# A cumulative sum behind a matrix product: the first 4 MB brought by hardware queues as float32

## The chip, the cores and the metric

The kernel runs on one core of a Trainium2 chip. The metric is device time in microseconds (us) of the whole launch, lower is better. Matrix work runs on TensorE (PE in the profile, its weight loads PEld), vector work on VectorE (DVE), ScalarE (ACT) and GpSimd (POOL). Transfers are issued by SyncE (SP) and ScalarE on hardware queues, and by GpSimd on a software queue that can also cast float32 to bf16 on the way.

## What is computed

```python
B, S, D = 16, 2048, 1024          # x: B x S x D, w: D x D, decay: D, all float32
xw = x @ w
out[:, 0, :] = xw[:, 0, :]
for t in range(1, S):
    out[:, t, :] = decay[None, :] * out[:, t - 1, :] + xw[:, t, :]
```

## The kernel before

x is cut along time into 64 chunks of TL = 512 steps. A chunk arrives as bf16 in `xb` (four transfers by GpSimd, one for each 32 partitions), is turned in 32x32 blocks on VectorE into `xw` (`turn`) and copied into `xt` (`part`), which is the moving operand of the matmuls. w lies in `wsb` as bf16, 8 blocks k of the contraction times 8 blocks n of output columns. Chunks are taken in pairs. A step of the main loop is one n for one pair: 8 k's, 128 x 512 matmuls into PSUM, then the scan over time on VectorE (half of the tiles with help of ScalarE and GpSimd), a turn back and a store by SyncE. What each engine does in which order is written out by hand in `agenda`, a string of letters for each step. A letter calls the function that `deeds` gives it, and `pin` holds each instruction behind the one before it in program order on its own engine.

The change lies in the opening, the entry -99 of `agenda` and the lines ahead of it. There w's two column halves (h) and x's first two chunks come in. In w, rows with an even k belong to e = 0 and with an odd k to e = 1, so (h, e) names a quarter of w, 1 MB in float32. The staging room is the memory of two output tiles, `room[0]` and `room[1]` (so the profile calls these tiles `ot`).

- Lines 339 to 341: SyncE and ScalarE each bring 128 full rows of x (float32, 512 KB): the first half of chunk 0, in `whole`.
- `U0` to `U3` (`load_part`, `load_w`, line 323): GpSimd brings a quarter of w, cast to bf16, in four transfers. `M1` to `M3` (`load_half`, `load`, line 105): GpSimd brings half a chunk of x in four transfers; M1 is the second half of chunk 0, M2 and M3 are chunk 1. GpSimd's order is U0, I1, M1, U1, M2, M3, U2, U3 (I1 makes the unit matrix `eye`), then the loads `L` of later chunks.
- `H` and `J` (`gather`, line 376): VectorE and ScalarE cast the float32 rows to bf16 and reorder them into `upright`. `t0` to `t3` (`erect`, line 386): TensorE transposes them, 4 x 128x128 each, into a PSUM bank (`bed`). `o` and `O` (`lay`, line 393): VectorE and ScalarE copy them to `xt`.
- Line 354: TensorE runs 12 matmuls on zeros (`spin`) at the start. `K0` to `K3` (`spin_on`, line 404): when a piece of w's first quarter is in, ScalarE copies one column into a gate tile, and TensorE runs two or three more spins that need it.
- `W` and `w` (`settle_one`, line 330), `q` and `Q` (line 419): VectorE and ScalarE copy staged w into `wsb`.
- `n0` and `n1` (`begin`): 16 matmuls of 256 columns each, even k's, on the first and on the second half of chunk 0. The second half was turned on VectorE (`E4` to `E7`).
- Step 0 of the loop then runs the odd k's of chunk 0 (16 matmuls of 512 columns), then all k's of chunk 1.
- `D` makes the decay columns from `rows` (line 356, four small transfers by SyncE).

Of the kernel before, what the change touches and what calls it, by code (L numbers as in the profile page):

```python
# [9 lines left out]
FP32 = mybir.dt.float32  # L10
BF16 = mybir.dt.bfloat16
# [3 lines left out]
def _ap(ap_obj: bass.AP, new_ap, extra_offset=0):  # L15
    return dataclasses.replace(
        ap_obj,
        ap=[list(p) for p in new_ap],
        offset=ap_obj.offset + extra_offset,
    )  # L20
# [5 lines left out]
def kernel(  # L26
# [26 lines left out]
    nc = tc.nc  # L53
    pin = tc.keep_in_program_order
    B, S, D = x.shape
    assert w.shape == (D, D)

    NQ = 4
    P = 32
    CQ = D // NQ  # L60
    K = CQ // P
    M = K // 2
    TL = 512
    NJ = TL // P
    NC = S // TL
    R = K // 2
    CH = D // 2
    CR = CH // NQ

    const = ctx.enter_context(tc.tile_pool(name="const", bufs=1))  # L70
    sb = ctx.enter_context(tc.tile_pool(name="sb", bufs=1))
# [4 lines left out]
    def ring(pool, name, count, shape, dtype=FP32):  # L76
        i = turns[name] = turns.get(name, -1) + 1
        return pool.tile(shape, dtype, name=f"{name}{i % count}")

    def quad(q):  # L80
        return slice(q * P, (q + 1) * P)
# [12 lines left out]
    def ot_tile(nj):  # L94
        return ring(sb, "ot", 4, [128, nj, CR])

    xb_of = {}
    xw_of = {}
    xt_of = {}
# [25 lines left out]
    def matmul(ps, n, k, xt, t0=0, t1=TL, start=0, pairs=None):  # L125
        if pairs is None:
            rhs = xt[:, k // 2, k % 2, t0:t1]
        else:
            rhs = pairs[:, k // 2, t0 // P:t1 // P, :, k % 2].rearrange("p j i -> p (j i)")
        lhs = wsb[:, k, n].rearrange("p q i -> p (q i)")  # L130
        pin(nc.tensor.matmul(  # L131
            out=ps[:, t0:t1] if ps.shape[1] >= t1 else ps,
            lhsT=lhs,
            rhs=rhs,
            start=(k == 0 and t0 == start),
            stop=(k == K - 1),
        ))
# [3 lines left out]
    class Tile:  # L141
# [39 lines left out]
        def copy(self):  # L181
            self.xs = sb.tile([128, 2 * TL], FP32, name=f"xs{self.lot % 3}")[:, 0:self.T]
            parts = self.ps if isinstance(self.ps, tuple) else (self.ps,)
            size = self.T // len(parts)
            for i, ps in enumerate(parts):
                pin(nc.scalar.copy(out=self.xs[:, i * size:(i + 1) * size], in_=ps))  # L186
# [103 lines left out]
    class Outlet:  # L290
# [8 lines left out]
        def store(self, b, t0, j0, j1):  # L299
# [4 lines left out]
            for j in range(j0, j1, nj):  # L304
# [8 lines left out]

    room = [ot_tile(2 * NJ).rearrange("p j c -> p (j c)") for _ in range(2)]
    size = M * CH
    stage = {(0, 0): room[0][:, 0:size // 2].bitcast(BF16),
             (0, 1): room[0][:, size:size * 3 // 2].bitcast(BF16),
             (1, 0): room[1][:, 0:size // 2].bitcast(BF16),
             (1, 1): room[1][:, size // 2:size].bitcast(BF16)}

    def load_w(queues, h, e):
        for i, q in enumerate((0, 2, 1, 3)):
            pin(queues[i % len(queues)].dma_start(  # L323
                out=stage[h, e][quad(q)].rearrange("p (m d) -> p m d", m=M),
                in_=_ap(w, [[2 * D, P], [2 * P * D, M], [1, CH]],
                        (q * CQ + e) * D + h * CH)))

    def settle(h, e, m, copy):
        src = stage[h, e][:, m * CH:(m + 1) * CH]
# [3 lines left out]
    idle = const.tile([128, TL], BF16, name="idle")  # L333
    spare = ring(psp, "spare", 1, [128, TL])
    rows = const.tile([128, 2, P], FP32, name="rows")
    touch = const.tile([128, 1], BF16, name="touch")
    H = NJ // 2
    halves = ((0, H), (H, NJ))
    whole = room[1][:, size:2 * size].rearrange("p (u c) -> p u c", u=2)
    for u, queue in enumerate((nc.sync, nc.scalar)):  # L340
        pin(queue.dma_start(out=whole[:, u], in_=_ap(x, [[D, 128], [1, D]], u * 128 * D)))
    pin(nc.vector.memset(idle, 0.0))  # L342
    pin(nc.vector.memset(rows, 0.0))
    pin(nc.scalar.copy(out=touch, in_=idle[:, 0:1]))

    gates = [const.tile([128, 128], BF16, name=f"gate{q}") for q in range(NQ)]
    for gate in gates:
        pin(nc.vector.memset(gate, 0.0))

    def spin(count, by):  # L350
        for _ in range(count):
            pin(nc.tensor.matmul(out=spare, lhsT=by, rhs=idle, start=True, stop=True))  # L352

    spin(12, idle[:, 0:128])
    for q in range(NQ):
        pin(nc.sync.dma_start(
            out=rows[q * P:q * P + R],
            in_=_ap(decay, [[P, R], [CH, 2], [1, P]], q * CR)))
    cols = const.tile([128, 2, P], FP32, name="cols")

    def load_half(i):
# [5 lines left out]
    firsts = [ps[:, 0:TL] for ps in heads] + [spares[0]]  # L367
    seconds = [ps[:, TL:2 * TL] for ps in heads] + [spares[1]]
    eye = const.tile([128, 128], BF16, name="eye")

    upright = room[0][:, size * 3 // 2:2 * size].bitcast(BF16).rearrange(
        "p (e u m c) -> p e u m c", e=2, u=2, m=M)

    def gather(i, copy):
        e, u = i // 2, i % 2
        pin(copy(out=upright[:, e, u].rearrange("p m (q i) -> p m q i", q=NQ),
                 in_=whole[:, u].rearrange(
                     "p (q m i e) -> p e m q i", q=NQ, m=M, e=2)[:, e]))

    def bed(e):  # L380
        return seconds[e].bitcast(BF16).rearrange("p (m t) -> p m t", m=M)

    def erect(i):
        e, u = i // 2, i % 2
        for m in range(M):
            pin(nc.tensor.transpose(
                out=bed(e)[:, m, u * 128:(u + 1) * 128], in_=upright[:, e, u, m], identity=eye))

    def lay(i, copy):
        e, m = i // 2, i % 2 * 2  # L390
        if 0 not in xt_of:
            xt_of[0] = ring(sb, "xt", 5, [128, M, 2, TL], BF16)
        pin(copy(out=xt_of[0][:, m:m + 2, e, 0:H * P], in_=bed(e)[:, m:m + 2]))

    def begin(i):
        for k in range(0, K, 2):
            for n in range(R):
                if i == 0:
                    matmul(firsts[n], n, k, xt_of[0], 0, H * P)
                else:  # L400
                    matmul(firsts[n], n, k, xt_of[0], H * P, TL, pairs=xw_of[0])

    def spin_on(q):
        pin(nc.scalar.copy(out=gates[q][quad(q), 0:1], in_=stage[0, 0][quad(q), 0:1]))
        spin(3 if q == 0 else 2, gates[q])

    def load_part(i):
        load_w((nc.gpsimd,), i // 2, i % 2)

    def part_one(i, copy):  # L410
        part(i // 8, copy, i % 4, i % 4 + 1, *halves[i // 4 % 2])
# [106 lines left out]
    def turn_and_load(c):  # L518
# [16 lines left out]
        "w": lambda i: settle_one(i, nc.scalar.copy),  # L535
        "M": load_half,
        "U": load_part,
        "E": lambda i: turn(i // 8, *halves[i // 4 % 2], i % 4, i % 4 + 1),
        "F": lambda i: part_one(i, nc.vector.tensor_copy),
        "G": lambda i: part_one(i, nc.scalar.copy),  # L540
        "K": spin_on,
        "t": erect,
        "H": lambda i: gather(i, nc.vector.tensor_copy),
        "J": lambda i: gather(i, nc.scalar.copy),
        "O": lambda i: lay(i, nc.scalar.copy),
        "o": lambda i: lay(i, nc.vector.tensor_copy),
        "n": begin,
        "q": lambda i: settle_slots(i, 0, 1),
        "Q": lambda i: settle_slots(i, 1, R),
# [19 lines left out]
        "L": lambda i: load(*loads.pop(0)) if loads else None,  # L569
    }  # L570
    agenda = {
        -99: "U0 I1 M1 U1 M2 M3 U2 U3 H0 J1 t0 t1 H2 J3 t2 t3 O1 o0 K0 O3 o2 K2 K1 K3 W0 W1 w2 W3 n0 E4 E5 G4 E6 G5 E7 F6 G7 n1 q4 w5 Q4 W6 W7 D E8 E9 G8 E10 G9 E11 F10 G11 E12 L E13 G12 L E14 G13 E15 L F14 G15",
        0: "p0 z0 W8 W9 W10 W11",
        1: "g0",
        2: "L S1 L",
# [88 lines left out]
    for step, (g, n) in enumerate(slots):  # L664
        T = TL * len(g)
        left = step - len(slots)
        if n % R == 0:
            ns, nj = range(n, n + R), T // P
            if left == -2 * R:
                outlets = [Outlet(ns, H, half) for half in range(2)]  # L670
            else:
# [4 lines left out]
        if step == 0:  # L676
# [3 lines left out]
            for k0 in range(0, K, 2):  # L680
                for i in range(R):
                    for k in (k0, k0 + 1):
                        matmul(seconds[i], i, k, xt_of[1], 0, H * P,
                               pairs=xw_of[1] if k0 < 4 else None)
            for i in range(R):
                for k in range(K):
                    matmul(seconds[i], i, k, xt_of[1], H * P, TL, H * P,
                           pairs=xw_of[1] if i < 2 else None)
        if step < R:
            ps = heads[n] if n < 3 else tuple(spares)  # L690
        else:
# [16 lines left out]
            elif step == K:  # L708
                todo = []
                nexts = (ring(psp, "spare", 1, [128, TL]), ring(psp, "ps", 3, [128, TL]))  # L710
                for l in range(len(g)):
                    for i, half in enumerate((ps[:, l * TL:(l + 1) * TL], nexts[l])):
                        for k in range(K):
                            matmul(half, n + i, k, xt_of.get(g[l]),
                                   pairs=xw_of[g[l]] if g[l] in (3,) else None)
# [51 lines left out]
```

## Time and profile before

| | |
|---|---|
| median of 3 runs | 904.07 us (903.53 to 904.18) |
| the profiled execution | 903.72 us |
| its span on the core | 901.9 us |
| PE busy | 891.2 us, 99% of the span |
| DVE, ACT, POOL busy | 823.5, 687.1, 657.2 us |
| first matmul of `begin` | 9.95 us |
| start of step 0's odd k's | 14.97 us |
| first out transfer of SyncE | about 38.4 us |

Times inside the kernel count from the start of the span. The span is what the instructions of the core cover; the rest of the profiled execution's time lies around it. In the timelines a row has the start, the time to the end of the last instruction merged into it, the engine, the line, what it writes and reads, how many, and in brackets how long the engine was idle before and what released it.

### The profile page before, as it was taken

Reading aid. Unit: us, or ns where it says so; the run is one execution under the profiler, and the core shown is the slowest. Engines: PE = TensorE matmul, PEld = TensorE weight load, DVE = VectorE, ACT = ScalarE, POOL = GpSimd, SP = SyncE. Lnnn points to the kernel's source line nnn. Section 1 sums busy time; section 2 is a strip of 40 time slices with the busy share of each in tenths; the row PEclk is TensorE's granted clock in tenths of the full one; section 3 lists DMA queues with packets and bytes.
Section 4 is the critical chain, followed back from the end, with each engine's and each line's share of the span. In section 5 each row is a group of like instructions: output and inputs, shape, how many; then the busy total and the mean of one; then the engine's idle time right before and its main releaser. Section 6 shows DMA issues by size and latency. Waiting matters only on the chain.

```text
span 901.9 us, 12229 instructions
## 1 busy us (share of the span) xinstructions
PE 891.2 (99%) x4131; PEld 411.9 (46%) x4213; DVE 823.5 (91%) x636; ACT 687.1 (76%) x962; POOL 657.2 (73%) x757
## 2 busy tenths in 40 slices
PE   8999999999999999999999999999999999999998
PEld 5544444444444444444444444444444444444444
DVE  4999998989999999999998999999999999999998
ACT  4889867778877877878778778777787787787743
POOL 8888678768767768677677687777777776876532
PEclk9999999999999999999999999999999999999999
DMA  9999999999999999999999999999999999999868
GB/s 193 195 215 218 229 212 207 216 233 247 247 248 255 248 255 252 246 254 250 222 235 228 218 236 227 233 226 227 232 230 227 227 236 222 226 228 221 177 153 231
DMA packets 402382, 204.77 MB, mean 227 GB/s; under 512 B 9360, under 2 KB 401552, under 8 KB 402320
## 3 DMA queue, kind: packets, MB, share of 16 engines
q1 hardware_dynamic: 265664, 134.77, 60.8%
q0 software_dynamic: 136512, 68.70, 56.8%
q8 instruction: 33, 0.54, 0.2%
q10 hardware_dynamic: 144, 0.52, 0.1%
q14 instruction: 29, 0.24, 0.1%
HBM read 138.42 MB, written 134.22 MB: 302 GB/s over the span
## 4 chain that ended last, share of the span: by engine, by line
PE 97%; DMA 1%; issue 1%; POOL 0%; DVE 0%; ACT 0%; DVEq 0%; POOLq 0%
PE ps L131 96%; PE spare L131 1%; DMA ot<-in_w_dram 1%; POOL ot L323 0%; DVE so L233 0%; PE ps L460 0%; PE spare L460 0%; ACT xb L467 0%; DVE wsb L419 0%; DVEq L419 0%; POOLq L751 0%
## 5 line engine op out<-in xcount | busy, mean ns | idle before, releaser
L131 PE MATMUL ps<-xt,wsb 128*128 128x512 bf16 (+1 forms) x3946 | 862.6, 378 | 4.7 <-DVE wsb L419 0.4
L131 PEld LDWEIGHTS <-wsb 128*128 128x128 bf16 x4160 | 406.5, 98 | 479.8 <-issue 0.9
L208 POOL TENSOR_TENSOR xs<-h,xs 128x512 f32<-128x512 f32 (+1 forms) x190 | 242.7, 1278 | 184.1 <-ACT h L169 83.1
L283 DVE STREAM_TRANSPOSE ot<-so 128x1024 f32<-128x1024 f32 (+2 forms) x265 | 300.2, 1171 | 6.5 <-DMA out_dram<-ot 4.4
L186 ACT COPY xs<-ps 128x1024 f32<-128x1024 f32 (+1 forms) x190 | 188.8, 994 | 149.3 <-PE ps L131 137.5
L266 POOL TENSOR_TENSOR so<-h,xs 128x512 f32<-128x512 f32 (+1 forms) x190 | 241.2, 1271 | 46.9 <-ACT h L169 27.2
L123 ACT COPY xt<-xw 128x2048 bf16<-128x2048 bf16 (+1 forms) x133 | 240.6, 1816 | 9.5 <-DVE xw L115 9.5
L105 POOL DMA_DIRECT2D xb<-in_x_dram x260 | 171.6, 661 | 2.9 <-DMA ot<-in_w_dram 0.9
L169 ACT ACTIVATE h<-so,dec 128x512 f32<-128x512 f32 (+1 forms) x190 | 145.3, 766 | 32.8 <-DVE so L213 29.9
L115 DVE STREAM_TRANSPOSE xw<-xb 128x2048 f32<-128x2048 f32 (+1 forms) x74 | 145.9, 1981 | 6.5 <-DMA xb<-in_x_dram 6.5
L213 DVE TENSOR_TENSOR_SCAN so<-spare,keep,xs 128x512 f32<-128x512 f32 (+1 forms) x97 | 119.8, 1237 | 25.9 <-POOL xs L208 25.6
L213 DVE TENSOR_TENSOR_SCAN so<-spare,xs 128x512 f32<-128x512 f32 x93 | 113.0, 1217 | 25.4 <-POOL xs L208 22.8
L169 ACT ACTIVATE h<-ps,dec 128x512 f32<-128x512 f32 (+1 forms) x189 | 129.3, 684 | 0.0
L233 DVE TENSOR_TENSOR_SCAN so<-dec,ps 128x1024 f32<-128x1024 f32 x34 | 76.9, 2260 | 0.8 <-ACT h L169 0.6
L233 DVE TENSOR_TENSOR_SCAN so<-dec,keep,ps 128x1024 f32<-128x1024 f32 (+2 forms) x35 | 74.7, 2138 | 0.0
L270 ACT COPY keep<-so 128x1 f32<-128x1 f32 x136 | 25.2, 188 | 9.1 <-DVE so L233 8.7
L204 ACT COPY so<-keep 128x1 f32<-128x1 f32 x97 | 18.4, 191 | 2.6 <-DVE ot L283 2.4
L131 PE MATMUL spare<-xt,wsb 128*128 128x512 bf16 (+1 forms) x68 | 14.0, 329 | 0.0
L323 POOL DMA_DIRECT2D ot<-in_w_dram x16 | 9.0, 561 | 2.9 <-POOLq L751 0.9
L202 POOL MEMSET so<- 128x1 f32 x93 | 10.7, 116 | 0.6 <-DVE ot L283 0.6
L131 PE MATMUL ps<-xw,wsb 128*128 128x256 bf16 (+1 forms) x56 | 9.3, 307 | 0.8 <-DVE xw L115 0.8
L352 PE MATMUL spare<-idle 128*128 128x512 bf16 x12 | 5.3, 632 | 1.2 <-DVE idle L342 1.2
(46 smaller groups left out, 43.9 us busy)
## 6 DMA issues: line engine op xcount, KB each, us to landing
out_dram<-ot SPq DMA_DIRECT2D x236, 512.0 KB, 10.8
xb<-in_x_dram POOLq DMA_DIRECT2D x248, 256.0 KB, 7.8
out_dram<-ot SPq DMA_DIRECT2D x56, 128.0 KB, 2.5
ot<-in_w_dram POOLq DMA_DIRECT2D x16, 128.0 KB, 5.6
out_dram<-ot SPq DMA_DIRECT2D x8, 256.0 KB, 4.2
xb<-in_x_dram POOLq DMA_DIRECT2D x12, 128.0 KB, 5.3
out_dram<-xb SPq DMA_DIRECT2D x4, 256.0 KB
ot<-in_x_dram ACTq DMA_DIRECT2D x1, 512.0 KB, 4.9
```

Source lines behind the costliest of these rows:

```text
L105: pin(nc.gpsimd.dma_start(out=xb_of[c][quad(q), j0:j1], in_=_ap(x, [[D, P], [P * D, j1 - j0], [1, CQ]], (b * S + t0 + j0 * P) * D + q * CQ)))
L115: pin(nc.vector.transpose(out=dst.rearrange("p (m j i) -> p j m i", m=M, i=P)[:, j0:j1, m0:m1], in_=src.rearrange("p (j m c) -> p j m c", ...
L123: pin(copy(out=xt_of[c][:, m0:m1, :, j0 * P:j1 * P], in_=src))
L131: pin(nc.tensor.matmul(out=ps[:, t0:t1] if ps.shape[1] >= t1 else ps, lhsT=lhs, rhs=rhs, start=(k == 0 and t0 == start), stop=(k == K - 1),))
L169: pin(nc.scalar.activation(out=h, in_=src, func=mybir.ActivationFunctionType.Copy, scale=dec[:, self.n:self.n + 1]))
L186: pin(nc.scalar.copy(out=self.xs[:, i * size:(i + 1) * size], in_=ps))
L208: pin(nc.gpsimd.tensor_tensor(out=odds, in0=self.g, in1=odds, op=ALU.add))
L213: pin(nc.vector.tensor_tensor_scan(out=so[:, 3:T + 2:2], data0=squares[-1][:, n:n + 1].to_broadcast([128, T // 2]), data1=self.xs[:, 1:T:2 ...
L233: pin(nc.vector.tensor_tensor_scan(out=so[:, t + 2:t + 2 + size], data0=dec[:, n:n + 1].to_broadcast([128, size]), data1=ps, initial=befor ...
L266: pin(nc.gpsimd.tensor_tensor(out=self.so[:, 2:T + 2:2], in0=self.h, in1=self.xs[:, 0:T:2], op=ALU.add))
L270: pin(nc.scalar.copy(out=self.keep, in_=self.so[:, self.T + 1:self.T + 2]))
L283: pin(nc.vector.transpose(out=outlet.ot[:, j:j + size, c0:c0 + P], in_=self.so[:, t1:t1 + size * P].rearrange("p (i t) -> p i t", t=P)))
```

## The change

The hardware queues bring, all as float32: the first half of chunk 0 (`load_rows`, as before), its second half the same way, and then the whole left column half of w (h = 0). Each of SyncE and ScalarE issues, after its first x rows, one more transfer of 512 KB of x rows and six of w (128 KB each for the even k's in two parts, 256 KB each for the odd k's). ScalarE's seven come after its small copy `touch` and before its first `J`. U0, M1 and U1 are gone from GpSimd's queue; after I1 it runs `v` (`hold`), a copy of two columns that needs both transfers of the second rows, and then M2, M3, U2, U3.

The second half of chunk 0 takes the same way as the first: cast and reordered (H4, J5, H6, J7), transposed on TensorE (t4 to t7), laid into `xt` (o4, O5, o6, O7). `begin` becomes four calls, n0 to n3, one even k each, with four matmuls of 512 columns. The gate copies and their spins are gone; five plain spins stand after t3 and one after t7. The first half's staging of w is float32, so its settles read float32. `upright` lies in chunk 0's `xw` tile and the second rows in its `xb` tile.

```diff
-    stage = {(0, 0): room[0][:, 0:size // 2].bitcast(BF16),
-             (0, 1): room[0][:, size:size * 3 // 2].bitcast(BF16),
+    stage = {(0, 0): room[0][:, 0:size],
+             (0, 1): room[0][:, size:2 * size],
...
-    for u, queue in enumerate((nc.sync, nc.scalar)):
-        pin(queue.dma_start(out=whole[:, u], in_=_ap(x, [[D, 128], [1, D]], u * 128 * D)))
+    xb_of[0] = ring(sb, "xb", 3, [128, NJ, CQ], BF16)
+    xw_of[0] = ring(sb, "xw", 2, [128, M, NJ, P, 2], BF16)
+    wholes = [room[1][:, size:2 * size],
+              xb_of[0].rearrange("p j c -> p (j c)").bitcast(FP32)]
...
+    def load_rows(queue, i, u):
+        pin(queue.dma_start(
+            out=wholes[i][:, u], in_=_ap(x, [[D, 128], [1, D]], (2 * i + u) * 128 * D)))
+
+    def load_rest(queue, u):
+        load_rows(queue, 1, u)
+        for e, m0, m1 in ((0, 0, 2), (0, 2, M), (1, 0, M)):
+            load_w(queue, 0, e, m0, m1, (u, u + 2))
+
+    load_rows(nc.sync, 0, 0)
+    load_rows(nc.scalar, 0, 1)
+    load_rest(nc.sync, 0)
     pin(nc.vector.memset(idle, 0.0))
     pin(nc.vector.memset(rows, 0.0))
     pin(nc.scalar.copy(out=touch, in_=idle[:, 0:1]))
+    load_rest(nc.scalar, 1)
...
-    upright = room[0][:, size * 3 // 2:2 * size].bitcast(BF16).rearrange(
-        "p (e u m c) -> p e u m c", e=2, u=2, m=M)
+    upright = xw_of[0].rearrange("p m j i e -> p (m j i e)").rearrange(
+        "p (h e u m c) -> p h e u m c", h=2, e=2, u=2, m=M)
...
     def begin(i):
-        for k in range(0, K, 2):
-            for n in range(R):
-                if i == 0:
-                    matmul(firsts[n], n, k, xt_of[0], 0, H * P)
-                else:
-                    matmul(firsts[n], n, k, xt_of[0], H * P, TL, pairs=xw_of[0])
-
-    def spin_on(q):
-        pin(nc.scalar.copy(out=gates[q][quad(q), 0:1], in_=stage[0, 0][quad(q), 0:1]))
-        spin(3 if q == 0 else 2, gates[q])
+        for n in range(R):
+            matmul(firsts[n], n, 2 * i, xt_of[0])
+
+    def hold(i):
+        pin(nc.gpsimd.tensor_copy(out=held, in_=wholes[1][:, :, 0:1].rearrange("p u c -> p (u c)")))
...
-        -99: "U0 I1 M1 U1 M2 M3 U2 U3 H0 J1 t0 t1 H2 J3 t2 t3 O1 o0 K0 O3 o2 K2 K1 K3 W0 W1 w2 W3 n0 E4 E5 G4 E6 G5 E7 F6 G7 n1 q4 w5 Q4 W6 W7 D ...",
+        -99: "I1 v M2 M3 U2 U3 H0 J1 t0 t1 H2 J3 t2 t3 O1 o0 O3 o2 K5 H4 J5 t4 t5 H6 J7 t6 t7 o4 O5 K1 W0 n0 o6 w1 n1 W2 O7 n2 W3 n3 q4 w5 Q4 W6 W7 D ...",
```

## The prediction

> **What bounds the kernel now.** I read the page first, for shares and for the chain that ended last.
>
> ```profile
> PE 891.2 (99%) x4131; PEld 411.9 (46%) x4213; DVE 823.5 (91%) x636; ACT 687.1 (76%) x962; POOL 657.2 (73%) x757
> ...
> PE 97%; DMA 1%; issue 1%; POOL 0%; DVE 0%; ACT 0%; DVEq 0%; POOLq 0%
> ```
>
> TensorE is the bound: 99% busy, 97% of the chain. The wait list of PE after 15 us has one entry, 0.4 us, which is the wait that ends at 14.97. So the odd-k half of step 0 starts at 14.97 and nothing stops PE from there on. The change edits only the opening, so its price is the shift of that start, provided the later waits stay away. To see what sets 14.97 I asked for the chain of the first 20 us (start, length, what).
>
> ```profile
> 1.31 1.25 POOL ot L323 x2
> 2.56 5.65 DMA ot<-in_w_dram
> 8.21 0.28 issue
> 8.50 0.54 POOL ot L323
> 9.04 0.13 issue
> 9.16 5.43 DMA ot<-in_w_dram
> ...
> 14.72 0.21 DVE wsb L419
> 14.92 0.05 issue
> 14.97 0.39 PE ps L131
> ```
>
> The start hangs on w's odd rows, landed at 14.60. Stranger is the step before: GpSimd could issue that transfer only at 8.50, because a transfer of w's even rows landed at 8.21. The two share no bytes. GpSimd's timeline shows the count behind it.
>
> ```profile
> 1.31 2.32 POOL L323 DMA_DIRECT2D ot<-in_w_dram  x4 [0.86 <-POOLq L751]
> ...
> 4.16 2.41 POOL L105 DMA_DIRECT2D xb<-in_x_dram  x4
> 6.88 0.55 POOL L323 DMA_DIRECT2D ot<-in_w_dram  x1 [0.31 <-DMA ot<-in_w_dram]
> 7.59 0.54 POOL L323 DMA_DIRECT2D ot<-in_w_dram  x1 [0.17 <-issue]
> 8.50 1.32 POOL L323 DMA_DIRECT2D ot<-in_w_dram  x2 [0.36 <-DMA ot<-in_w_dram]
> ```
>
> Eight transfers go out freely (4 + 4); the ninth waits for the first to land, the eleventh for the third. So a completion semaphore is reused after eight transfers, and the issuing engine stands until its previous user has landed. The operands recorded in the trace say the same of the hardware queues: their 310 transfers use eight semaphores in rotation, SyncE's and ScalarE's in one ring (the ninth, an output of SyncE at 39.44, carries and waits for the semaphore of ScalarE's one x transfer). Before, only six hardware transfers run in the opening, so this ring never bites.
>
> **The change part by part.** *Transfers.* The first 4 MB move from "1 MB float32 on hardware, then 3 MB source cast on GpSimd's queue" to hardware alone. DMA rows (window, ..., share, GB/s):
>
> ```profile
> 3.00:4.50 1.50, 1.50 (x5) 0.48 (x4) 0.00 (x0) 0.00 (x0) 1.42 (x5) 1.00 1.04 421
> 10.00:11.50 1.50, 1.50 (x16) 1.34 (x15) 0.00 (x0) 0.00 (x0) 1.01 (x2) 1.00 1.39 189
> ```
>
> Hardware moves 421 GB/s of float32. The cast queue's 189 GB/s are bf16 written, so 378 read. Hence 4.19 MB take 10.0 us on hardware; with flow from about 2.4 (GB/s is 66 until 2.5) the last byte is there at 12.4 if nothing stops the issue. [...]
>
> *Seven transfers on ScalarE ahead of its first gather (J1).* Each costs 0.41 us of issue at most (the row of its x transfer). That would be hidden: 7 x 0.41 from 2.67 (end of `touch`) ends at 5.5, and J1 starts at 5.65. But SyncE and ScalarE now issue 16 transfers before the decays, in a ring of eight. ScalarE is in order, so J1, J3, O1 and all its later copies queue behind its last issue, and t1 on PE behind J1. When is that last issue? If the two engines alternate in the ring, the sixteenth waits for the eighth, a piece of w's first half: 2.10 MB of x rows and 0.52 MB of w must land. 2.4 + 2.62 MB / 421 GB/s = 8.6, plus 0.6 from last byte to landing (x rows: about 4.9 to 5.45) = 9.2, plus issue: J1 starts at 9.6. If SyncE's eight come first in the ring, the last issue waits for its last w pieces, and J1 comes at about 10.9. The lower bound is 5.65, no wait. I take 9.6, between and nearest to GpSimd's row, where every wait for the eighth-last is paid in full.
>
> *From J1 to the first matmul.* J1 and J3 take 1.21 together: 9.6 to 10.8. From J1's end to O1 took 0.93 before (5.65 + 0.65 to 7.23): O1 at 11.2, O3 0.57 later and after t3, about 12.0 to 12.5. On DVE o0 began at 7.84 when ACT's O1 ended ("<-ACT xt L393", 1.62); likewise o2 now follows O3: 12.4 to 12.8. H4 and H6 follow at 0.44 each, H4 ends 13.25. Then 0.93 again to o4 (14.2), 0.42 for it, and W0, now float32 to bf16, between 0.28 (DVE's bf16 copy) and 0.44 (H); I take 0.42. First matmul T = 15.05. The sixteen 512-column matmuls of n0 to n3 take what the same count took from 14.97 to 18.43, 3.46 us, so the odd half starts at 18.5. w1, W2, W3 and O7 lie beside those matmuls (0.62 or less each against 0.87 for a group of four). W's odd rows have then long landed (last issue 9.6, plus 4.9 as for the x rows).
>
> *Spins and clock.* The opening spins run at 0.43 us each (5.30 for 12); those at 7.95 at 0.24 (2.16 for 9). Now PE has nothing but t0 between the spins' end (6.5) and t1 (10.3). If it falls back to the slow pace, the five spins of K5 take 2.1 instead of 1.2 and end after H4: 0.75 late, and eight transposes cost 0.05 more each (weight load 0.15 against 0.098): 1.1 in all. If not, 0. I take half, 0.5. Sum: 18.5 + 0.5 - 14.97 = +4.0.
>
> *Removed.* The gate copies and nine gate spins, none in the chain. *GpSimd's `hold`* stops M2, M3, U2, U3 and the loads behind them until both x rows of the second half land, about 8 (11 with SyncE first in the ring). Eight then go out freely; M2 took 7.6 from first issue to use (9.86 to 17.49), so chunk 1's first turn can run at 15.6 to 18.8, and PE wants it at about 22. Hidden; without that cover each us late is a us. Chunk 1 and w's other half come earlier relative to PE than now. SyncE's decays wait in the ring too, but `D` runs after the odd settles.
>
> **Forecast.** The profiled execution took 903.72 (span 901.9 and 1.8 around it), the median of the runs 904.07, 0.35 more. +4.0 on 903.72 is 907.7; on the median, 908.1. Its own range is +2.2 (J1 at 9.0, no slow clock, W0 0.28, o4 not behind o2) to +5.9 (J1 at 10.9, slow clock): 906.3 to 910.0. A difference of 0.2%, 1.8 us, is about what a measurement of this kernel can tell from none.
>
> **Rivals.** *No wait on ScalarE (no change).* If the ring's order leaves ScalarE's seven behind transfers already landed, J1 stays near 5.65 and o2 ends at 8.82 as now. H4 to 9.26, o4 10.19, W0 done 11.05, T = 11.1: 11.1 + 3.46 - 14.97 = -0.4, 903.7. W's odd rows must land by 14.2 (12.4 + 0.6, beside M2). For it: the ring is seen biting only on GpSimd. Against it: the shared rotation in the operands. *Faster.* Without the wait, and if the O/o pairs did not queue behind each other (the 1.62 us row), H4 could start as the rows land, near 8.0, and T reach 9.7 or less: that is where -1.8 begins, 902.2. Needs the rows 0.4 us sooner than 421 GB/s gives. Not likely. *Clock longer slow.* If PE stays at 0.43 through n0 to n3, 8 to 16 matmuls cost 0.21 more each, on top of the whole 1.1: 3.5 + 1.1 + 1.7 to 3.4 = +6.3 to +8.0, 910.4 to 912.1. Before, the slow pace lasted over five us of busy PE, which t1 to K5 nearly fill. [...]
>
> **Chances.** Forecast 0.60; no wait 0.22; long slow clock 0.12; faster 0.06. Slower by over 0.2%: 0.60 + 0.12 = 0.72; within: 0.22; faster: 0.06. The range goes from 903.3 (most of the no-wait case) to 911.2, which leaves out the faster case, the tail of no-wait and half of the slow-clock case.
>
> **What would show it.** ScalarE's DMA issues on the second x rows' line spread over 2.7 to about 9, with waits on DMA landings; its first gather cast at 9 to 11 instead of 5.65; PE idle before the second group of transposes; the first real matmul at 14.5 to 16, the odd half of step 0 at 18 to 20; no PE wait after it. Wrong if ScalarE's gathers start near 5.7, or if PE waits for chunk 1's turns or for w's odd rows.

## The result, and the profile after

The kernel after takes 909.33 us (median of 4 runs, 908.76 to 909.63) against 903.87 us (903.53 to 904.18) before: ratio 1.0061, 95% interval [1.0046, 1.0075], slower by 5.46 us. The profiled execution took 909.63, its span 907.9.

The page's busy row and its chain by engine:

```profile
PE 897.7 (99%) x4210; PEld 412.7 (45%) x4210; DVE 825.3 (91%) x631; ACT 687.2 (76%) x959; POOL 650.7 (72%) x746
PE 98%; DMA 1%; ACT 0%; ACTq 0%; DVE 0%; issue 0%
```

TensorE is still the bound. The chain of the first 30 us of the kernel after (start, length, what) shows how its opening hangs together:

```profile
1.67 0.45 ACTq L323
...
2.15 8.85 DMA ot<-in_w_dram
...
11.02 0.32 ACTq L323
...
11.38 0.65 ACT xw L391
...
12.07 1.46 PE ps L401 x12
13.54 2.13 PE spare L366 x5
```

A transfer of w, issued at 2.15 and landed at 11.00, releases no reader of its bytes. It releases another DMA issue of ScalarE, and only then does ScalarE run J1, the cast of x rows that had landed by 5.9 (DVE's half of that work, H0, starts at 5.71). This is GpSimd's picture of before, on the hardware queues and with an engine behind it that also has arithmetic to do. ScalarE's timeline, with the idle time before a row and its releaser in brackets:

```profile
1.67 1.12 ACTq L323 DMA_DIRECT2D ot<-in_w_dram  x2
2.48 0.19 ACT L361 COPY touch<-idle 128x1 bf16<-128x1 bf16 x1
5.71 5.63 ACTq L323 DMA_DIRECT2D ot<-in_w_dram  x4
11.38 1.19 ACT L391 CAST xw<-ot 128x512 bf16<-128x512 f32 x2 [8.71 <-DMA ot<-in_w_dram]
```

Four transfers issue freely (with the two of x rows), then the other four take from 5.71 to 11.34. The semaphores recorded with the issues alternate between ScalarE and SyncE, eight in rotation: ScalarE's last transfer waits for its own fourth, the eighth in the ring, which landed at 11.00. More rows of the same opening, from TensorE's timeline:

```profile
12.07 1.46 PE L401 MATMUL ps<-eye,xw 128*128 128x128 bf16 x12 [5.19 <-ACT xw L391]
13.33 2.34 PE L366 MATMUL spare<-idle 128*128 128x512 bf16 x5
...
17.38 0.82 PE L131 MATMUL ps<-xt,wsb 128*128 128x512 bf16 x3
...
20.84 0.81 PE L131 MATMUL ps<-xt,wsb 128*128 128x512 bf16 x3
```

After 5.19 us of idle time the five spins take 2.34, 0.43 each. The first matmul of `begin` is at 17.38 (9.95 before), and the odd half at 20.84 instead of 14.97: +5.87, with no wait of PE after it. The profiled times differ by 909.63 - 903.72 = 5.91, so the opening is the whole loss. Last, the stretches of 1 us (window, length, busy time of the five engines, granted clock, DMA share, GB/s):

```profile
7.00:8.00 1.00, 0.00 (x0) 0.00 (x0) 0.00 (x0) 0.00 (x0) 0.00 (x0) 1.00 1.04 412
8.00:9.00 1.00, 0.00 (x0) 0.00 (x0) 0.00 (x0) 0.00 (x0) 0.02 (x1) 1.00 1.08 260
9.00:10.00 1.00, 0.00 (x0) 0.00 (x0) 0.00 (x0) 0.00 (x0) 0.58 (x2) 1.00 1.08 238
10.00:11.00 1.00, 0.00 (x0) 0.00 (x0) 0.00 (x0) 0.00 (x0) 1.00 (x3) 0.57 1.07 236
11.00:12.00 1.00, 0.00 (x0) 0.00 (x0) 0.00 (x0) 0.62 (x2) 1.00 (x2) 0.50 1.08 238
```

While x rows move, 412 GB/s; once only w moves, 236 to 238, at the same full DMA share. The granted clock falls to 0.50 in the same time.

### The profile page after: what moved, and what is told of

Read it like the earlier page. It is cut to its first block, busy times and chain, and to the rows that moved or that the text cites. A ratio compares the mean times of both kernels' runs of the same rounds, so it can differ in the third digit from the quotient of the medians.

```text
span 907.9 us, 12302 instructions
## 1 busy us (share of the span) xinstructions
PE 897.7 (99%) x4210; PEld 412.7 (45%) x4210; DVE 825.3 (91%) x631; ACT 687.2 (76%) x959; POOL 650.7 (72%) x746
## 4 chain that ended last, share of the span: by engine, by line
PE 98%; DMA 1%; ACT 0%; ACTq 0%; DVE 0%; issue 0%
PE ps L131 96%; PE spare L131 1%; DMA ot<-in_w_dram 1%; PE spare L366 0%; PE ps L401 0%; DVE so L233 0%; ACTq L323 0%; PE spare L401 0%; ACT xw L391 0%; PE ps L472 0%; ACT L361 0%; PE spare L472 0%; ACTq L348 0%; ACT xb L479 0%
## 5 line engine op out<-in xcount | busy, mean ns | idle before, releaser
L131 PE MATMUL ps<-xt,wsb 128*128 128x512 bf16 x4028 | 868.3, 378 | 0.0
L105 POOL DMA_DIRECT2D xb<-in_x_dram x256 | 169.3, 662 | 2.0 <-DVE xw L115 0.9
L131 PE MATMUL spare<-xt,wsb 128*128 128x512 bf16 (+1 forms) x68 | 14.5, 335 | 0.0
L366 PE MATMUL spare<-idle 128*128 128x512 bf16 x18 | 8.0, 618 | 1.2 <-DVE idle L359 1.2
L401 PE MATMUL ps<-eye,xw 128*128 128x128 bf16 x24 | 3.1, 311 | 5.2 <-ACT xw L391 5.2
```

What stands on the lines that cost most here:

```text
L105: pin(nc.gpsimd.dma_start(out=xb_of[c][quad(q), j0:j1], in_=_ap(x, [[D, P], [P * D, j1 - j0], [1, CQ]], (b * S + t0 + j0 * P) * D + q * CQ)))
L131: pin(nc.tensor.matmul(out=ps[:, t0:t1] if ps.shape[1] >= t1 else ps, lhsT=lhs, rhs=rhs, start=(k == 0 and t0 == start), stop=(k == K - 1),))
```

## The experiments

The theories: **(1)** the shared ring of eight holds ScalarE up; **(2)** w flows at little more than half the rate, so the landing that ScalarE waits for is late; **(3)** the slow pace after idle adds about 1 us. The rivals: the order in which w lands would set the time without any wait on ScalarE, or x's half of the change is the costly one. The edits below are to the kernel after. SyncE and ScalarE have u = 0 and 1 in `load_rest`; the w pieces lie in four groups of 32 partitions. The intervals reach about 1.4 us to either side, so a difference of a microsecond or less between two experiments is not settled by their medians alone; it is read from the traces with them.

### Experiment 1: ScalarE's w transfers issued by SyncE (e1_sp_issues)

```diff
     def load_rest(queue, u):
         load_rows(queue, 1, u)
-        for e, m0, m1 in ((0, 0, 2), (0, 2, M), (1, 0, M)):
-            load_w(queue, 0, e, m0, m1, (u, u + 2))
+
+    def load_left(queue):
+        for e, m0, m1 in ((0, 0, 2), (0, 2, M), (1, 0, M)):
+            load_w(queue, 0, e, m0, m1, (0, 1, 2, 3))
...
     load_rest(nc.scalar, 1)
+    load_left(nc.sync)
```

> The changed kernel with ScalarE's six w transfers issued by SyncE instead (ScalarE keeps only its two x rows). Ring theory: ScalarE no longer stands, J1 back at about 5.7, rows laid as they land (8.4 and 8.9), first real matmul near 11; but w still comes at the 238 GB/s that the changed kernel's rows show from 8 to 13, 7.6 + 2.10 MB / 238 = 16.4, landed 17.0, odd half at 17.4 instead of 20.84: 909.3 - 3.4 = 905.9 us. Rival (ScalarE is late for another reason, or the slow w transfers alone set the start): odd half stays at 20 to 21, 908.5 to 909.5.

Measured: 909.15 us (907.33 to 910.72) against 903.71; ratio 1.0059 [1.0044, 1.0074]. ScalarE's and TensorE's timelines of this kernel, the latter's rows from two places:

```profile
5.71 1.21 ACT L394 CAST xw<-ot 128x512 bf16<-128x512 f32 x2 [3.04 <-DMA ot<-in_x_dram]
```

```profile
11.48 0.82 PE L131 MATMUL ps<-xt,wsb 128*128 128x512 bf16 x3 [0.78 <-DVE wsb L331]
...
18.98 1.46 PE L131 MATMUL ps<-xt,wsb 128*128 128x512 bf16 x3 [3.32 <-DVE wsb L434]
...
25.39 0.84 PE L131 MATMUL ps<-xw,wsb 128*128 128x256 bf16 x6
```

J1 is back at 5.71 and the first matmul at 11.48, 5.9 earlier than in the kernel after: the ring does what (1) says. The time hardly moves all the same: 5.44 above its before, where the kernel after is 5.46 above. The runs spread from 907.33 to 910.72, and the rows are those of the longest. In it the odd half waits 3.32 us for w's odd rows, landed at 18.57. It still starts 1.86 before that of the kernel after, but in the wait the granted clock has gone to 0.50, and the sixteen matmuls take 6.41 us (18.98 to 25.39) where the kernel after takes 3.46. So 1.86 are won and 2.95 lost, and the profiled execution ends 1.09 above that of the kernel after.

The expectation in time was missed by 3.2 us, and the time lies where the rival had it. The expectation had the rate of w in it (238 GB/s, landed at 17.0), and the rate came: 219 to 238 from 9 to 13 us, with a single queue. It had no price for what a wait of TensorE does to its clock. And the rows landed 1.57 later still: from 13 to 18 us GpSimd's transfers, chunk 1 above all, move beside them, and their packets take 56% of the DMA engines' time.

### Experiments 2, 3 and 9: which partitions are written together

```diff
# e2_swapped: ScalarE's two groups in the other order, (3, 1)
-            load_w(queue, 0, e, m0, m1, (u, u + 2))
+            load_w(queue, 0, e, m0, m1, ((0, 2), (3, 1))[u])
# e3_fewer: even rows in one piece of 256 KB, 12 transfers ahead of J1
-        for e, m0, m1 in ((0, 0, 2), (0, 2, M), (1, 0, M)):
+        for e, m0, m1 in ((0, 0, M), (1, 0, M)):
# e9_halves: as e3, SyncE with groups 0 and 1, ScalarE with 2 and 3
+            load_w(queue, 0, e, m0, m1, (2 * u, 2 * u + 1))
```

> The changed kernel with ScalarE's w pieces in the order of partition groups 3, 1 instead of 1, 3, so that the two queues never fill the same half of the partitions at one time. If the 238 GB/s come from both queues writing the same 64 partitions: w flows at about 420, the eighth landing moves from 11.0 to about 9.5, J1 from 11.4 to 9.9, time -1.5: 907.8. [...]

> The changed kernel with w's even rows in one transfer of 256 KB per partition group instead of two of 128 KB: 12 instead of 16 hardware transfers ahead of the decays, same bytes in nearly the same order. Ring theory: ScalarE's last issue now waits for the fourth transfer (second x rows, 8.86) instead of the eighth (11.0): J1 at 9.2, first matmul 6.0 later at 15.2, odd half 18.7, time -2.1: 907.2. Rival (bytes or issue cost, not the count in flight): J1 stays at 11 or later, 909.3.

> e3_fewer (12 transfers, 256 KB each) with SyncE bringing w's partition groups 0 and 1 and ScalarE groups 2 and 3, so that each queue always writes its own half of the partitions (before: 0 and 2, 1 and 3, with 0 and 1 at one time). If two queues on the same 64 partitions make the 230 to 240 GB/s: rate 350 to 420 from 8 on, odd rows landed by 14.5 instead of 18.0, no wait of PE at 18; J1 at 9.0 as in e3, odd half at 17.8 or so, 906.3 to 906.7 against e3's 907.2. Rival (a piece over 32 partitions is slow whatever the other queue does): 230 to 290 GB/s as in e3 and e2, 907.2.

Measured: e2 908.78 us (908.52 to 908.97), ratio 1.0056 [1.0041, 1.0071]; e3 907.16 (907.02 to 907.21), 1.0038 [1.0023, 1.0053]; both against 903.71. e9 906.44 (906.35 to 907.24) against 903.74, 1.0032 [1.0020, 1.0044].

In the kernel after, SyncE's groups are 0 and 2 and ScalarE's 1 and 3, so the two queues write groups 0 and 1 at one time and 2 and 3 at the next, always in the same 64 partitions. The stretches of e3, which keeps those groups, and then of e9, where each queue has its own 64:

```profile
8.00:9.00 1.00, 0.00 (x0) 0.00 (x0) 0.00 (x0) 0.00 (x0) 0.19 (x1) 1.00 1.03 233
9.00:10.00 1.00, 0.27 (x5) 0.27 (x6) 0.00 (x0) 0.96 (x2) 0.58 (x1) 1.00 1.01 227
```

```profile
8.00:9.00 1.00, 0.00 (x0) 0.00 (x0) 0.00 (x0) 0.00 (x0) 0.19 (x1) 1.00 1.06 375
9.00:10.00 1.00, 0.27 (x5) 0.28 (x6) 0.00 (x0) 0.97 (x2) 0.61 (x1) 1.00 1.05 358
```

With the same number, size and order of transfers, only the partitions differ (and with them which rows of w are read at one time), and the rate goes from 227 to 233 up to 358 to 375 GB/s. The packets are 2 KB in both, so their size is not the reason. Theory (2) has its cause: transfers that are under way together in one half of the partitions.

What it buys depends on what is late. In e3 and e9 alike the twelfth transfer waits for the fourth, x rows, so J1 is at 9.04 and 9.03 and the first matmul at 14.38 and 14.35. In e3 the odd half then waits for w's odd rows (18.43); in e9 it does not (17.81). TensorE's rows at the odd half, of e3 first, then of e9:

```profile
18.43 0.87 PE L131 MATMUL ps<-xt,wsb 128*128 128x512 bf16 x3 [0.43 <-DVE wsb L431]
```

```profile
17.81 0.81 PE L131 MATMUL ps<-xt,wsb 128*128 128x512 bf16 x3
```

That is the difference of 0.7 us in time. e9 came as expected, but that its odd rows landed at 15.05 and not by 14.5, which was still in time. e3 has the expected time, in part by luck: the first matmul came 0.8 earlier than expected, and the wait for the odd rows, which was not expected, gave most of it back. e3 also answers the first rival: it changes the count of transfers and not the rate, and the time falls by 2.17. e2 pairs group 0 with 3 and 2 with 1, and still gets only 281 to 295 GB/s from 8 to 11 us: J1 10.74 instead of 11.38, and the time 0.55 less, a third of what I had expected of it. The landings suggest why: ScalarE's pieces land 0.2 to 0.3 us behind SyncE's (9.58 and 10.36 after 9.28 and 10.16), and 0.8 to 0.9 us apart within a queue, so for part of the time the two are in the same half after all. No run shows that this is the reason.

### Experiment 4: TensorE kept busy (e4_warm)

```diff
-... H0 J1 t0 t1 H2 J3 ...
+... H0 J1 t0 K20 t1 H2 J3 ...
```

> The changed kernel with 20 more plain spins between t0 and t1 on PE, so that PE is busy until about 11.7 while it waits for J1. If the slow pace of K5 and of the second transposes (0.43 a spin) comes from PE's idle 5.2 us: K5 runs at 0.22 to 0.24 a spin, t4 follows H4, transposes 0.05 shorter each: odd half 0.6 to 1.0 earlier, 908.3 to 908.7. Rival (the pace does not depend on the idle time, or K5 is not in the way): 909.3 or later.

Measured: 908.30 us (908.02 to 908.62) against 903.71; ratio 1.0052 [1.0035, 1.0068]. TensorE's timeline, with the twenty added spins and then the five of K5:

```profile
6.05 4.48 PE L366 MATMUL spare<-idle 128*128 128x512 bf16 x20
...
12.53 1.24 PE L366 MATMUL spare<-idle 128*128 128x512 bf16 x5
...
15.79 0.82 PE L131 MATMUL ps<-xt,wsb 128*128 128x512 bf16 x3 [0.19 <-DVE wsb L331]
```

K5 takes 1.24 instead of 2.34, a hit for (3). J1 is at 11.05, and from there to the first matmul it is 4.74 instead of 6.00: the slow pace was worth 1.26. The profile's chain for this run has W0 wait for a transfer of w landed at 15.33. That one was issued at 9.67, ScalarE's fifth of w, and brings odd rows, where W0 reads even ones. VectorE's timeline shows W0 0.34 behind the copy ahead of it, the same distance as from W0 to the copy that follows:

```profile
14.98 0.42 DVE L409 COPY xt<-ps 128x512 bf16<-128x512 bf16 x1 [0.39 <-PE ps L401]
15.32 0.42 DVE L331 CAST wsb<-ot 128x512 bf16<-128x512 f32 x1
15.65 0.42 DVE L409 COPY xt<-spare 128x512 bf16<-128x512 bf16 x1
```

So W0 waited for no transfer, and 4.74 is the chain at full pace. With J1 0.33 earlier the first matmul comes 1.59 earlier, and the profiled execution, 908.05, is 1.58 below that of the kernel after; the 0.33 are not the spins' doing, since x's rows and the eighth transfer landed about that much earlier in this run.

### Experiment 5: without the hold on GpSimd's queue (e5_no_hold)

```diff
-... "I1 v M2 M3 U2 U3 H0 ...
+... "I1 M2 M3 U2 U3 H0 ...
```

> The changed kernel without GpSimd's wait (the copy of two columns is left out): chunk 1's eight transfers go out from about 1.5 instead of 9.6. If the queues share the engines, rows and w are pushed back by part of the 2.1 MB read for chunk 1: J1 at 12.5 to 14, 910.5 to 912. Rival (hardware transfers of 4 KB packets go first, as before the change, where the cast queue moved nothing until 4.8): J1 as it is, 909.3, or a little earlier use of chunk 1 that PE does not feel.

Measured: 910.34 us (909.76 to 911.05) against 903.80; ratio 1.0070 [1.0054, 1.0085]. GpSimd's timeline, of the kernel after first, then of this one:

```profile
8.98 0.18 POOL L417 COPY held<-xb 128x2 f32<-128x2 f32 x1 [7.67 <-DMA xb<-in_x_dram]
9.58 4.72 POOL L105 DMA_DIRECT2D xb<-in_x_dram  x8 [0.42 <-issue]
```

```profile
1.51 4.89 POOL L105 DMA_DIRECT2D xb<-in_x_dram  x8 [0.19 <-issue]
```

Chunk 1's eight transfers go out 8.1 us earlier, and the hardware queues are slower beside them: 267 and 256 GB/s from 6 to 8 us, where the kernel after has 401 and 412. J1 slips to 12.88, inside the stretch expected, and the first matmul to 18.75; the time is 0.16 below the range expected. From 2 to 9 us the cast queue's packets took only 8% of the DMA engines' time, so why they cost the others so much stays open. The hold is worth about 1.0 us; it costs nothing, since TensorE never waits for chunk 1 in the kernel after.

### Experiments 6 and 7: w over all partitions, then also with ScalarE freed

In both, w's left half comes in eight transfers over 128 partitions. The rows of w then lie in other partitions than the products need; only the time is read.

```diff
# e6_wide, in load_rest
-        for e, m0, m1 in ((0, 0, 2), (0, 2, M), (1, 0, M)):
-            load_w(queue, 0, e, m0, m1, (u, u + 2))
+        for e in range(2):
+            for m in (u, u + 2):
+                load_wide(queue, e, m)    # 128 partitions, 2 KB each
# e7_wide_sp: e = 0 alone in load_rest, and behind it
+    for m in range(M):
+        load_wide(nc.sync, 1, m)
```

> The changed kernel with w's first half brought in eight transfers over all 128 partitions (256 KB each, 2 KB packets) instead of twelve over 32 partitions each; the rows of w land in other partitions than the product needs, so only its time is read. 12 hardware transfers ahead of the decays as in e3_fewer. If the 32-partition destinations make the 230 to 240 GB/s: w at 380 to 420, odd rows landed at about 13.5, first matmul as in e3 (14.4), odd half at 17.9 without a wait, 906.6 against e3's 907.2. Rival (2 KB packets or the ring make the rate): rate stays at 240, odd rows at 17 to 18, 907.2.

> e6_wide with both causes taken away: ScalarE issues its two x rows and two pieces of w that the ring has free, SyncE the rest (w's rows again in other partitions, so only the time is read). J1 at 5.7 by the ring theory, first matmul near 11.2 (e1 had 11.48), w's odd rows landed near 13.5, odd half at 14.7: 903.4 to 903.9, no change against the kernel before. Rival (a further cause, clock or contention with chunk 1's loads): odd half later than 16, 905 or more.

Measured: e6 909.06 us (908.59 to 909.71) against 903.80, ratio 1.0058 [1.0045, 1.0072]. e7 903.18 (902.86 to 904.09, 11 runs) against 903.80, 0.9993 [0.9984, 1.0002].

e6 missed in time. The rate came, 348 to 406 GB/s from 9 to 12 us, but its ring did not: three of SyncE's four small decay transfers took slots ahead of ScalarE's last one, which so waited for a piece of w (10.84), and J1 came at 11.23. A fast w alone buys nothing while ScalarE stands in the ring, just as in e1 a free ScalarE bought no time while w was slow and the clock fell in the wait for it. e7 does both. The chain of its first 19 us ends at another place:

```profile
1.25 7.07 DMA xb<-in_x_dram
...
9.09 1.88 POOL xb L105 x3
10.96 7.41 DMA xb<-in_x_dram
...
18.51 0.46 DVE xw L115
```

TensorE's timeline:

```profile
14.22 0.81 PE L131 MATMUL ps<-xt,wsb 128*128 128x512 bf16 x3
...
19.01 0.84 PE L131 MATMUL ps<-xw,wsb 128*128 128x256 bf16 x6 [0.98 <-DVE xw L115]
```

J1 is at 6.16, the first matmul at 10.76 and the odd half at 14.22, 0.75 earlier than before the change and 0.5 earlier than expected. TensorE then gives 0.98 back, waiting for the first turn of chunk 1, whose transfer the hold released. So the two causes together, with the slow pace that rides on the waits they make, are the loss of 5.5 us: with both away 903.18 is no more than 0.6 below the kernel before, inside the interval.

### Experiment 8: x's half of the change alone (e8_rows_only)

```diff
     def load_rest(queue, u):
         load_rows(queue, 1, u)
-        for e, m0, m1 in ((0, 0, 2), (0, 2, M), (1, 0, M)):
-            load_w(queue, 0, e, m0, m1, (u, u + 2))
...
-... "I1 v M2 M3 U2 ...
+... "U0 I1 U1 M2 M3 U2 ...     # w in bf16 by GpSimd's queue, as before
```

> One part of the change alone: x's second rows by the hardware queues and TensorE as in the changed kernel, but w cast by GpSimd as before (U0, U1, then M2, M3; no wait on GpSimd). Four hardware transfers, so the ring never bites. w's even rows start when the rows are through (7.6): landed near 11, odd rows near 13.8; first matmul 11.4, odd half 14.9: 903.6 to 904.2, no change. Rival (x's way over TensorE costs by itself): 905 or more.

Measured: 904.06 us (903.38 to 905.65, 11 runs) against 903.80; ratio 1.0006 [0.9997, 1.0015]. A hit by the median: x's second rows over hardware and TensorE cost nothing that can be measured there. So the loss is w's six transfers per queue, which answers the second rival. With only four hardware transfers of x the ring of eight never fills, and J1 is at 5.60.

The profiled execution is the longest of the eleven, 905.65, and is not as expected: first matmul 11.96, odd half 17.11.

```profile
11.96 1.24 PE L131 MATMUL ps<-xt,wsb 128*128 128x512 bf16 x3 [1.34 <-DVE wsb L331]
12.98 0.63 PE L131 MATMUL spare<-xt,wsb 128*128 128x512 bf16 x1
13.41 1.49 PE L131 MATMUL ps<-xt,wsb 128*128 128x512 bf16 x3
...
17.11 0.81 PE L131 MATMUL ps<-xt,wsb 128*128 128x512 bf16 x3
```

After a wait of 1.34 us for w's even rows the granted clock goes to 0.50 and the first matmuls run at 0.43 each. The sixteen of n0 to n3 take 5.15 us instead of 3.46, and 1.69 more is about what this execution lies above the median. Two others of the eleven are at 905.5, the remaining eight at 903.4 to 904.3. So x's half of the change costs nothing in most executions and can cost about 1.6 us by the slow pace.

### Experiments 10 to 12: odd rows of w behind J1

```diff
# e10_free: as e9, the odd rows of ScalarE issued after O3
+    load_odd(nc.sync, 0)
...
-... O1 o0 O3 o2 K5 ...
+... O1 o0 O3 l o2 K5 ...     # l: load_odd(nc.scalar, 1)
# e11_free_no_hold: e10 without v
# e12_decays_late: e10 with the four decay transfers written after o2
+... O1 o0 O3 l o2 r K5 ...   # r: the decay transfers
```

> A complete kernel without both causes: w's pieces as in e9, and only eight hardware transfers ahead of ScalarE's first gather (w's odd rows follow: two on SyncE, two on ScalarE after O3, when the ring has landed). J1 at 5.7, first matmul 10.8 to 11.5, odd half 14.2 to 15.0, then possibly a wait of up to 1 us for chunk 1's turn as in e7: 902.9 to 904.0, the kernel before within 0.1%. Rival (w's odd rows still late): 905 or more.

> e10 without GpSimd's wait. In the changed kernel the wait was worth 1.0 us because J1 hung on w's landing; here chunk 1's use is next, so its earlier transfers should give back the wait that e7 had at 18 us (1.0), against x's second rows and w later by part of chunk 1's bytes: 902.4 to 904.4. If it is slower than e10 by 0.5 or more, the rows are still what the start hangs on.

> As in the run of halves with the odd w behind J1, but SyncE's four transfers of the decays are issued after ScalarE's two of the odd w, so that these stand in the ring behind x's rows (which landed at 8.1 and 8.5 us) and not behind a piece of w (11.15). If that place alone held ScalarE up there: the second of them is issued at about 8.5 instead of 11.17, J5 runs at about 9 instead of 11.53, the first matmul of begin is at about 11, the odd half at 14.3 to 14.8, within 0.7 us of its start before the change, and the time is 903.2 to 904.1. If it was the rate of w or the slow pace of TensorE that set the time: the odd half stays behind 17 and the time at 906.5 to 907.1. In between if the odd w, issued earlier, still lands after 16.

Measured: e10 907.11 us (906.81 to 907.60), ratio 1.0038 [1.0025, 1.0050]; e11 908.60 (908.48 to 909.24), 1.0056 [1.0044, 1.0069]; both against 903.74. e12 907.16 (906.83 to 907.96) against 903.79, 1.0039 [1.0025, 1.0053]. ScalarE's timeline of e10:

```profile
5.75 1.22 ACT L394 CAST xw<-ot 128x512 bf16<-128x512 f32 x2 [3.06 <-DMA ot<-in_x_dram]
...
8.16 3.34 ACTq L323 DMA_DIRECT2D ot<-in_w_dram  x2
11.53 1.19 ACT L394 CAST xw<-xb 128x512 bf16<-128x512 f32 x2 [3.49 <-DMA ot<-in_w_dram]
```

e10 frees J1 and J3, and the wait comes back one step on: ScalarE's second odd transfer stands in the ring behind SyncE's decays, on the slot of a w piece that landed at 11.15, and J5 waits with it. Missed by 3 us. e12 was to move those decays back. Its time lies by the second branch of what was expected (906.5 to 907.1), but the condition of neither was made: the recorded semaphores come in the same order as in e10, although the text issues the decays later, and J5 is at 11.78. So it is open what e10 would give with its ring in the other order. e11 says once more what the hold is for: without it 1.5 us more, which was the second branch of its expectation; its range, 902.4 to 904.4, was missed with that of e10.

No version here beat the kernel before by more than its measurement can tell; e7, the only one below it, does not lay w where the product needs it.

## Why the prediction was right in kind, and what was mis-sized

The forecast was 908.1, the result 909.33, on the side and by the mechanism that it named.

**The ring.** Right, to the detail: order alternating, ScalarE's last transfer waiting for the eighth. e1 shows it by taking the issues away (J1 from 11.38 to 5.71). The rival of no wait on ScalarE falls with it.

**J1 at 9.6: the term that was mis-sized.** It came at 11.38, 1.78 later and past my upper end of 10.9. Of the working, "2.62 MB / 421 GB/s" failed: the 421 is the row of x rows over all 128 partitions, and I used it for pieces of 32 partitions. Once only w moves the rate is 236 to 238. x's rows were late too: they landed at 8.38 and 8.84, where I had them by about 8. From 8.84 to the eighth landing, 11.00, it is 2.16 where my sum has 1.2 (8.0 to 9.2). So of the 1.78 about 1.0 is w's rate and about 0.8 the late rows. e9 shows where the rate comes from: with the number, size and order of e3's transfers it gets 358 to 375 GB/s from 8 to 10 us where e3 gets 227 to 233, and only the partitions that are written together differ (and the rows of w that are read with them).

**From J1 to the first matmul.** Forecast 5.45, and 0.5 as half of the slow pace; measured 6.00. The sum is right by luck, the parts are not. That TensorE would go back to the slow pace in its wait, and the half for it, was my estimate: no trace of before shows it, where the longest wait of PE is 1.2 us. Here, after 5.19 us, the spins of K5 took 0.43 each at a granted clock of 0.50. Shorter waits did it as well: in the profiled runs of e10 and e8 the clock went to 0.50 after 2.94 and 1.34 us. In e4 and e7 it stayed at 1.00 after 1.22 and 0.98. What decides it these runs do not show. The slow pace was paid in full, 1.26 where I had 1.1 for the whole of it, and the chain without it was shorter than the 5.45 that I had built up: 4.74 in e4.

**n0 to n3.** 3.46 forecast, 17.38 to 20.84 measured: 3.46. The clock was back at 1.00 by then, from 16.96 on, so the rival of a slow clock in these matmuls falls, though the time is near its 910.4.

**The sum.** The odd half was forecast at 19.0 with the clock, came at 20.84: 1.84 late, of which J1 is 1.78. On the profiled execution that is 909.63 against 907.7. That 909.33 still lies inside the forecast's own 906.3 to 910.0 is in part luck: J1 came 0.48 past the upper end used there, and the way from J1 took 0.55 less than the 6.55 that the upper end has with the whole slow pace.

**W's odd rows.** "Long landed" (9.6 plus 4.9, so 14.5) was wrong. VectorE's first copy of them:

```profile
19.37 0.59 DVE L431 CAST wsb<-ot 128x128 bf16<-128x128 f32 x2 [1.00 <-DMA ot<-in_w_dram]
```

The last of them landed at 19.25, 4.8 later than forecast and only 1.6 before TensorE took them up at 20.84. No wait showed because J1 was late as well. It is this term that comes to the front when J1 is freed, in e1 and e3.

**The hold.** Called hidden: so it was. That it would be worth 1.0 us I had not said. The warning that without cover each us late is a us is e7's wait of 0.98.

**The landings.** They moved a great deal by two things, the partitions that the two queues wrote together (w's last odd rows landed at 18.02 in e3 and at 15.05 in e9) and the ring (J1 at 11.38 in the kernel after and at 5.71 in e1).

**What would show it.** ScalarE's spread issues and PE's idle time before the second transposes were as named; J1, the first matmul and the odd half each lie up to 1.4 past the stretches given, by the late J1 and the slow pace.

## What to carry to other kernels

Before moving transfers onto an engine that also computes, count the transfers in flight over all hardware queues: past the eighth, here, an issue waits for a landing, and everything later on that engine waits with it (ScalarE's last issue until 11.02, and J1 until 11.38). Let the two queues write different halves of the partitions (358 to 375 GB/s in e9 against 227 to 233 in e3), and take a rate only from a row of the same shape (412 with x rows, 236 to 238 with w alone). When taking away the wait on the chain changes little, look for the second one just behind it before dropping the theory: by the medians, each against its before, the ring's wait removed alone brought 0.0 us here (e1), the slow rate alone 0.2 (e6), and both together 6.1 (e7). And price a wait of TensorE with what it does to the clock: in e1 the start won 1.86 us, and the slow matmuls behind the wait lost 2.95.

## What the runs showed of the hardware

- Two hardware queues that write the same 64 partitions moved 227 to 238 GB/s together (e3, the kernel after), each its own 64 partitions 358 to 377 (e9), at the same DMA share of 1.0 to 1.1. One queue that brings pieces of 32 partitions in order moved 219 to 238 (e1). The share alone does not show the loss; GB/s beside it does.
- The opening's twelve spins took 5.30 us, 0.43 each for the most part, while the stretches print a granted clock of 1.00. Later, 0.43 went with a recorded 0.50. The trace's first clock record stands at 6.72 us in the kernel after, so ahead of it the printed clock is no guide to the pace.
- Once at 0.50, the recorded clock stayed there for 3.41 us (e3, e8, e9, e10, e12) or 6.83 us (the kernel after, e1, e2, e5, e6, e11), also when TensorE was busy again before that.
- The order in which transfers get the eight semaphores is not the order of the program's text (e10 and e12 have the same), and it decides which landing an engine waits for: in both ScalarE stands until a piece of w has landed (11.15 and 11.39), with J5 at 11.53 and 11.78.
